# Fill for the last differential head from the output projection, in an encoder layer on one core

## The chip, the cores and the metric

The kernel runs on one core of one Trainium2 chip. The metric is the device time of one execution in microseconds, as the median of three runs.

## The reference

One layer of an encoder on a sequence of 512 tokens of width 2048, in float32: an input projection shared by two groups of attention heads, one output projection, and a SwiGLU network. Both halves are normed, shifted, scaled and gated by a condition `c`.

```
mod = silu(c) @ w_ada + b_ada;  sh1, sc1, gt1, sh2, sc2, gt2 = split(mod, 6)
h = rms_norm(x, g_norm1) * (1 + sc1) + sh1
q_d, k_d, v_d, cq, ckv, k_pe = split(h @ w_in)
a_out = rms_norm(differential_attention(norm(q_d), norm(k_d), v_d, lam, rel_bias))   # 8 heads, two softmaxes each
q_m = rms_norm(cq) @ w_q_b;  k_nope, v_m = split(rms_norm(ckv) @ w_kv_b)
b_out = latent_attention(rope(norm(q_m)), rope(norm([k_nope, k_pe])), v_m)            # 8 heads
x = x + gt1 * (concat(a_out, b_out) @ w_out)
h2 = rms_norm(x, g_norm2) * (1 + sc2) + sh2
x = x + gt2 * ((silu(h2 @ w_gate) * (h2 @ w_up)) @ w_down)
```

## The kernel before

All large products are made of three: each float32 operand is split into a high part and a low part (type fp32r), and `mm3` (L241) issues high by high, low by high and high by low into one PSUM bank. Such a **triple** of 512 columns is the unit in which this text counts. Activations lie transposed, 16 k-tiles of 128 x 512; the tokens are four row blocks of 128.

**Weights.** `weight_plan` lists all weight chunks in the order in which TensorE uses them. `Weights.get` hands out chunk i, splits chunk i+1 (ScalarE casts the high part, L90; VectorE or POOL subtracts for the low part, L98) and has SP load chunk i+2 (L74, L78). There are three raw buffers and two of each part. The output weights alternate between VectorE and POOL for the low part (`OUT_SPLIT`), those of the latent projections go to POOL.

**Order of the work.** TensorE keeps the order in which the program is written (`ORDERED`); for the other engines a scheduler chooses at build time. Attention runs head by head through lists of steps: `DIFF_STEPS` for the eight differential heads, `MLA_STEPS` for the eight latent heads. In them s, t, v, o, e and n are the scores of a row block, the transposes of the probabilities, the product with the values, the operands of the next head, the transposes of the finished output of the head before, and the start of the next head's norms. F and F1 are places for other work. There `between` lets a `Filler` take products from `projections` until so many microseconds of them are issued (`DIFF_FILL`, `MLA_FILL`, split over the places of a head), and lets `side_work` take one or two steps. A step of the side work in the latent heads loads a 128 x 512 piece of w_ada (L308) and accumulates it on VectorE (L312, L315): the second modulation's scales and shifts, 39 steps for each group of four k-tiles.

**What `projections` yields.** First what is left of the input projection, then `latents`, then for each of four pairs of latent heads `mla_project` (16 triples of 384 columns for the queries, 8 of 512 for keys and values). `out_half(b)` is the part of the output projection's column block b that needs only the differential heads: k-tiles 0 to 7, 32 triples, into the four banks of `acc`, and for b = 2 and 3 copied out into four slots (`half`). Before, it stands behind pairs 1 and 3. After each pair the generator yields 0, which ends a filling place, until the pair's first head has started and the last differential head's output exists:

```
if pr in (1, 3):
    yield from out_half({1: 2, 3: 3}[pr])
while pr not in started or mixT[H - 1] is None:
    yield 0
```

`mixT[H - 1]` is made in step e of the first latent head. Behind the last pair comes `out_half(0)`; behind the last head `fill.finish` issues all that is left, and the other parts of the output projection follow. The step lists run one head behind for t and v: a latent head's stretch, from its first score product to that of the next, holds its own scores, the transposes and values of the head before and the operands of the next.

**Buffers.** `slot` tiles (2 KB per partition, `N_SLOTS` of them) hold x, the split activations, operands, outputs, the halves and the pieces of w_ada.

Of the kernel before, what the change touches and what calls it, by code (L numbers as in the profile page):

```python
# [32 lines left out]


ORDERED = {mybir.EngineType.PE}
N_SLOTS = 45
T2_BUFS = 4
FIRST = 5

# [98 lines left out]
def weight_plan(a):  # L138
    w_in = a["w_in"][0]
    qkv = w_in[:, 0:3 * H * P].rearrange("(k p) (s n) -> p k s n", p=P, s=3)  # L140
    plan = []

    def rows(w, r0, nk, c0, n):
        return w[r0:r0 + nk * P, c0:c0 + n].rearrange("(k p) n -> p k n", p=P)

    def add_in(h, j):
        plan.append((("in", h, j), [2, 384], qkv[:, 2 * j:2 * j + 2, :, h * P:(h + 1) * P],
                     "dve" if h < FIRST else "pool"))

    for k0, nk in BLOCKS:  # L150
        for h in range(FIRST):
            for j in range(k0 // 2, (k0 + nk) // 2):
                add_in(h, j)
    for h in range(FIRST, H):
        for j in range(KC // 2):
            add_in(h, j)
    c0 = 3 * H * P
    for i in range(2):
        for j in range(KC // 4):
            plan.append((("cq", i, j), [4, 256], rows(w_in, j * 512, 4, c0 + i * 256, 256), "pool"))  # L160
    for j in range(KC // 2):
        plan.append((("ckv", j), [2, 320], rows(w_in, j * 256, 2, c0 + QL, 320), "pool"))

    def add_out(b, j0, j1):
        for j in range(j0, j1):
            plan.append((("out", b, j), [2, 512], rows(a["w_out"][0], j * 256, 2, b * 512, 512), OUT_SPLIT if j < 4 and b != 1 else "dve"))

    for pr in range(4):
        for j in range(2):
            plan.append((("qb", pr, j), [2, 384], rows(a["w_q_b"][0], j * 256, 2, pr * 384, 384), "pool"))  # L170
        plan.append((("kvb", pr), [2, 512], rows(a["w_kv_b"][0], 0, 2, pr * 512, 512), "pool"))
        if pr == 1:
            add_out(2, 0, 4)
        elif pr == 3:
            add_out(3, 0, 4)
    add_out(0, 0, 8)
    add_out(1, 0, 8)
    add_out(2, 4, 8)
    add_out(3, 4, 8)

    for j in range(STRAIGHT):
        for k4 in range(4):
            for n in ("gate", "up"):
                plan.append(((n, j, k4), [4, 256], rows(a["w_" + n][0], k4 * 512, 4, j * 256, 256), "dve"))
    return plan
# [14 lines left out]
def hybrid_layer(ctx, tc, a, out):  # L200
# [758 lines left out]
    def out_half(b):  # L959

        pss = [bank("acc", "ps_o") for _ in range(NT)]
        yield from project(pss, mixT, 512, [("out", b, j) for j in range(4)], 0, H, last=(b > 1), fine=True)
        if b > 1:
            half[b] = [slot("half", F32) for _ in range(NT)]
            for t in range(NT):
                act.copy(out=half[b][t], in_=pss[t])
        else:
            half[b] = pss
# [11 lines left out]
    def projections():  # L980
# [9 lines left out]
        yield from latents()  # L990
        for pr in range(4):
            yield from mla_project(pr)
            if pr in (1, 3):
                yield from out_half({1: 2, 3: 3}[pr])
            while pr not in started or mixT[H - 1] is None:
                yield 0
        yield from out_half(0)

# [473 lines left out]
GATE_EARLY = True  # L1472
START_FILL = 5.2
DIFF_STEPS = "s0 F s1 n F t0 F e s2 v0 F t1 F s3 v1 F t2 F o0 v2 t3 F o1 v3 F"
DIFF_FILL = (26.0, 26.0, 26.0, 26.0, 26.0, 26.0, 26.0, 26.3)
DIFF_SIDE = (1, 2, 1, 2, 1, 2, 1, 1)
MLA_SIDE = (1, 2)
MOD_EARLY = 8
MOD_PACE = (2.0, 2.4, 2.7, 1.5)
MLA_STEPS = "s0 F t0 e F1 t1 s1 v0 F t2 F1 v1 t3 s2 F v2 F1 o0 v3 F o2 o3 s3 o1 F1"  # L1480
MLA_FILL = (16.0, 15.7, 16.0, 0.2, 14.1, 19.0, 3.3, 12.8)


_INS = ["x", "c", "rel_bias", "w_ada", "b_ada", "g_norm1", "w_in", "g_q_diff", "g_k_diff", "lambda_vecs", "g_subln",
# [35 lines left out]
```

## Time and profile before

| | |
|---|---|
| three runs | 2253.54, 2254.41, 2261.16 us; median 2254.41 us |
| profiled execution | 2254.27 us, its span 2252.5 us |
| TensorE busy | 2178.6 us, 97% of the span |
| VectorE busy | 1648.1 us, 73% |
| ScalarE busy | 942.6 us, 42% |
| POOL busy | 262.7 us, 12%, all of it in the first 975 us |
| granted TensorE clock, mean | 0.996 of full speed |

Attention lies between about 200 and 755 us of the span, the latent heads from 542 us on. The network behind it takes the rest, with TensorE busy throughout. A busy TensorE says little by itself: the ends of matmuls are modelled, and a share over the whole span hides stretches of some 20 us. The windows view gives busy time, idle time as what is left, and the granted clock for stretches of one's own choice; those below begin and end with a head's first score product.

### The profile page before, as it was taken

The page shows a single profiled execution, that of the slowest core. Times are in us where ns is not written, and L with a number is a line of the kernel's source. Part 1 is how long each engine was busy: PE and PEld are TensorE (multiplying, and loading weights), DVE is VectorE, ACT ScalarE, POOL GpSimd, SP SyncE. Part 2 cuts the span into 40 slices and gives each one's busy share as a digit, 9 for nine tenths or more (in the row PEclk, how much of TensorE's full clock was granted, in tenths as well). Part 3 has the DMA queues.
Part 4 walks back from the last instruction along what each step waited for, and adds up shares of the span by engine and source line. Part 5 has one row for each costly group of instructions (what it writes and reads, how often), then busy time and mean ns, then how long its engine had stood idle before and what let it go on. Part 6 is the DMA issues. An engine that isn't in the chain of part 4 may idle for free.

```text
span 2252.5 us, 35369 instructions
## 1 busy us (share of the span) xinstructions
PE 2178.6 (97%) x13906; PEld 2000.5 (89%) x13906; DVE 1648.1 (73%) x2362; ACT 942.6 (42%) x1567; POOL 262.7 (12%) x408
## 2 busy tenths in 40 slices
PE   3899999998989999999999999999999999999999
PEld 3899998998777788899999999999999888888887
DVE  5997888868988687867777777777777677443554
ACT  4434555566555334534444444444444522221221
POOL 0003444345554000000000000000000000000000
PEclk9999999999999999999999999999999999999999
DMA  9995355422442684523333333333334686333443
GB/s 284 302 292 169 83 154 158 134 87 86 158 139 96 247 295 159 159 85 118 117 118 117 132 122 122 114 118 116 122 123 131 219 296 224 99 127 99 154 149 103
DMA packets 270826, 345.00 MB, mean 153 GB/s; under 512 B 15005, under 2 KB 171142, under 8 KB 270530
## 3 DMA queue, kind: packets, MB, share of 16 engines
q1 hardware_dynamic: 267864, 338.18, 46.5%
q10 hardware_dynamic: 2794, 4.55, 0.5%
q8 instruction: 109, 1.79, 0.3%
q14 instruction: 59, 0.48, 0.1%
HBM read 322.71 MB, written 19.96 MB: 152 GB/s over the span
## 4 chain that ended last, share of the span: by engine, by line
PE 67%; DVE 1%; DMA 0%; ACT 0%; issue 0%; POOL 0%; SPq 0%; DVEq 0%
PE ps_d L243 7%; PE ps_d L244 7%; PE ps_d L242 7%; PE ps_X L1285 5%; PE ps_X L1283 5%; PE ps_X L1284 5%; PE ps_W L1285 3%; PE ps_W L1283 3%; PE ps_W L1284 3%; PE ps_Y L1285 2%; PE ps_Z L1285 2%; PE ps_o L242 2%; PE ps_o L244 2%; PE ps_o L243 2%; PE ps_Y L1283 2%; PE ps_Z L1283 2%
## 5 line engine op out<-in xcount | busy, mean ns | idle before, releaser
L90 ACT CAST hi<-raw 128x1024 fp32r<-128x1024 f32 (+2 forms) x228 | 221.2, 970 | 479.2 <-PE ps_d L243 262.7
L98 DVE TENSOR_TENSOR lo<-raw,hi 128x1024 fp32r<-128x1024 f32 (+2 forms) x215 | 242.6, 1129 | 217.3 <-ACT hi L90 213.5
L1266 ACT CAST wh<-wr 128x1024 fp32r<-128x1024 f32 x160 | 168.2, 1051 | 245.3 <-PE ps_X L1284 69.2
L1285 PE MATMUL ps_X<-comb,wl 128*128 128x256 f32 x960 | 269.4, 281 | 0.0
L1283 PE MATMUL ps_X<-comb,wh 128*128 128x256 f32 x960 | 268.6, 280 | 0.0
L1284 PE MATMUL ps_X<-comb,wh 128*128 128x256 f32 x960 | 267.1, 278 | 0.0
L1249 DVE TENSOR_TENSOR wl<-wr,wh 128x1024 fp32r<-128x1024 f32 x160 | 195.6, 1222 | 76.5 <-ACT wh L1266 76.2
L244 PE MATMUL ps_d<-lo,ax 128*128 128x512 f32 x640 | 249.0, 389 | 0.0
L243 PE MATMUL ps_d<-hi,ax 128*128 128x512 f32 x640 | 249.0, 389 | 0.0
L242 PE MATMUL ps_d<-hi,ax 128*128 128x512 f32 x640 | 249.0, 389 | 0.0
L242 PE MATMUL ps_in<-hi,hh 128*128 128x384 f32 (+2 forms) x704 | 234.9, 334 | 3.3 <-ACT hh L397 1.3
L243 PE MATMUL ps_in<-hi,hl 128*128 128x384 f32 (+2 forms) x704 | 229.2, 326 | 4.3 <-DVE hl L403 4.3
L244 PE MATMUL ps_in<-lo,hh 128*128 128x384 f32 (+2 forms) x704 | 229.2, 326 | 3.4 <-DVE lo L98 3.4
L1266 ACT CAST wh<-wt 128x1024 fp32r<-128x1024 f32 x120 | 126.4, 1053 | 196.0 <-PE ps_X L1284 118.5
L1249 DVE TENSOR_TENSOR wl<-wt,wh 128x1024 fp32r<-128x1024 f32 x120 | 146.7, 1223 | 80.5 <-ACT wh L1266 80.3
L1283 PEld LDWEIGHTS ps_X<-comb,wh 128*128 128x128 f32 x960 | 180.5, 188 | 0.0
L1284 PEld LDWEIGHTS ps_X<-comb,wh 128*128 128x128 f32 x960 | 180.5, 188 | 0.0
L1285 PEld LDWEIGHTS ps_X<-comb,wl 128*128 128x128 f32 x960 | 180.2, 188 | 0.0
L1285 PE MATMUL ps_W<-comb,wl 128*128 128x256 f32 x640 | 179.6, 281 | 0.0
L1283 PE MATMUL ps_W<-comb,wh 128*128 128x256 f32 x640 | 179.2, 280 | 0.0
L1284 PE MATMUL ps_W<-comb,wh 128*128 128x256 f32 x640 | 178.1, 278 | 0.0
L242 PEld LDWEIGHTS ps_d<-hi,ax 128*128 128x128 f32 x640 | 120.2, 188 | 25.0
(324 smaller groups left out, 5330.6 us busy)
## 6 DMA issues: line engine op xcount, KB each, us to landing
raw<-in_w_down_dram SPq DMA_DIRECT2D x88, 512.0 KB
araw<-in_w_ada_dram SPq DMA_DIRECT2D x80, 512.0 KB
wr<-in_w_gate_dram SPq DMA_DIRECT2D x40, 1024.0 KB
wr<-in_w_up_dram SPq DMA_DIRECT2D x40, 1024.0 KB
ada<-in_w_ada_dram SPq DMA_DIRECT2D x128, 256.0 KB
raw<-in_w_in_dram SPq DMA_DIRECT2D x128, 192.0 KB
raw<-in_w_out_dram SPq DMA_DIRECT2D x32, 512.0 KB
x<-in_w_ada_dram SPq DMA_DIRECT2D x64, 256.0 KB
```

The lines of the kernel that those rows point to most:

```text
L90: nc.scalar.copy(out=hi[:, :n], in_=raw[:, :n])
L98: e.tensor_tensor(out=lo[:, :n], in0=raw[:, :n], in1=hi[:, :n].bitcast(F32), op=ALU.subtract)
L242: pe.matmul(o, ah, bh, start=start, stop=False)
L243: pe.matmul(o, al, bh, start=False, stop=False)
L244: pe.matmul(o, ah, bl, start=False, stop=stop)
L1249: dve.tensor_tensor(out=out, in0=x, in1=y, op=ALU.subtract)
L1266: act.copy(out=hi, in_=src)
L1283: pe.matmul(ps[bk], wh[:, k], c[:, 0], start=first and k == 0, stop=False, skip_group_check=True)
L1284: pe.matmul(ps[bk], wh[:, k], c[:, 1], start=False, stop=False, skip_group_check=True)
L1285: pe.matmul(ps[bk], wl[:, k], c[:, 0], start=False, stop=k == 7, skip_group_check=True)
```

## The change

`out_half(2)` moves from behind the second pair to behind the first, `out_half(3)` from behind the fourth to behind the third. The first of them no longer waits for the last differential head as a whole: it issues the triples of about six of its eight k-tiles, those that need the outputs of heads 0 to 5, and then yields 0 until the eighth head's output exists. The wait behind each pair is now only for its first head to start. `DIFF_FILL` of the last differential head rises from 26.3 to 38 us, `MLA_FILL` has other numbers. `N_SLOTS` is 51 instead of 45, and the kernel asks for a DMA scratch of 1024 bytes.

```diff
--- before.py
+++ after.py
@@ -33,7 +33,7 @@
 
 
 ORDERED = {mybir.EngineType.PE}
-N_SLOTS = 45
+N_SLOTS = 51
 T2_BUFS = 4
 FIRST = 5
 
@@ -169,9 +169,9 @@
         for j in range(2):
             plan.append((("qb", pr, j), [2, 384], rows(a["w_q_b"][0], j * 256, 2, pr * 384, 384), "pool"))
         plan.append((("kvb", pr), [2, 512], rows(a["w_kv_b"][0], 0, 2, pr * 512, 512), "pool"))
-        if pr == 1:
+        if pr == 0:
             add_out(2, 0, 4)
-        elif pr == 3:
+        elif pr == 2:
             add_out(3, 0, 4)
     add_out(0, 0, 8)
     add_out(1, 0, 8)
@@ -990,9 +990,16 @@
         yield from latents()
         for pr in range(4):
             yield from mla_project(pr)
-            if pr in (1, 3):
-                yield from out_half({1: 2, 3: 3}[pr])
-            while pr not in started or mixT[H - 1] is None:
+            if pr == 0:
+                first, due = out_half(2), 0.0
+                for t in first:
+                    yield t
+                    due += t
+                    while due > 6 * 12 * 512 * 0.000424 - 1 and mixT[H - 1] is None:
+                        yield 0
+            elif pr == 2:
+                yield from out_half(3)
+            while pr not in started:
                 yield 0
         yield from out_half(0)
 
@@ -1472,13 +1479,13 @@
 GATE_EARLY = True
 START_FILL = 5.2
 DIFF_STEPS = "s0 F s1 n F t0 F e s2 v0 F t1 F s3 v1 F t2 F o0 v2 t3 F o1 v3 F"
-DIFF_FILL = (26.0, 26.0, 26.0, 26.0, 26.0, 26.0, 26.0, 26.3)
+DIFF_FILL = (26.0, 26.0, 26.0, 26.0, 26.0, 26.0, 26.0, 38.0)
 DIFF_SIDE = (1, 2, 1, 2, 1, 2, 1, 1)
 MLA_SIDE = (1, 2)
 MOD_EARLY = 8
 MOD_PACE = (2.0, 2.4, 2.7, 1.5)
 MLA_STEPS = "s0 F t0 e F1 t1 s1 v0 F t2 F1 v1 t3 s2 F v2 F1 o0 v3 F o2 o3 s3 o1 F1"
-MLA_FILL = (16.0, 15.7, 16.0, 0.2, 14.1, 19.0, 3.3, 12.8)
+MLA_FILL = (21.0, 4.0, 21.0, 16.0, 16.5, 7.0, 5.0, 5.0)
 
 
 _INS = ["x", "c", "rel_bias", "w_ada", "b_ada", "g_norm1", "w_in", "g_q_diff", "g_k_diff", "lambda_vecs", "g_subln",
@@ -1504,7 +1511,7 @@
     import concourse.bacc as _bacc
     from concourse.bass_utils import run_bass_kernel_spmd as _run
 
-    nc = _bacc.Bacc("TRN2", target_bir_lowering=False, num_devices=1)
+    nc = _bacc.Bacc("TRN2", target_bir_lowering=False, num_devices=1, dynamic_dma_scratch_size=1024)
     arrays, aps = {}, {}
     given = {n: np.ascontiguousarray(inputs[n]) for n in _INS}
     given.update(_constants())
```

**TensorE, the end of the last differential head** (ps_s: scores, ps_z: product with the values, ps_aT: transposed probabilities, ps_qT and ps_kT: operands of the first latent head, ps_o: output projection). Before:

```order
L756 MATMUL ps_z<-v,aTh 128x256 x4
L759 MATMUL ps_z<-v,aTl 128x128 x4
L749 MATMUL ps_aT<-ident,pm 128x128 x4
L726 MATMUL ps_s<-k_5873,q_5865 128x512
L727 MATMUL ps_s<-klo,q_5865 128x512
L726 MATMUL ps_s<-k_6006,q_5998 128x512
L727 MATMUL ps_s<-klo,q_5998 128x512
L756 MATMUL ps_z<-v,aTh 128x256 x4
L759 MATMUL ps_z<-v,aTl 128x128 x4
L749 MATMUL ps_aT<-ident,pm 128x128 x4
L903 MATMUL ps_qT<-ident,qm 128x128 x4
L903 MATMUL ps_kT<-ident,kn 128x128 x4
```

After, from the same value product of the first row block (L759 behind the third score step) on:

```order
L759 MATMUL ps_z<-v,aTl 128x128 x4
L242 MATMUL ps_o<-hi,mh 128x512
L243 MATMUL ps_o<-hi,ml 128x512
L244 MATMUL ps_o<-lo,mh 128x512
L242 MATMUL ps_o<-hi,mh 128x512
L243 MATMUL ps_o<-hi,ml 128x512
L244 MATMUL ps_o<-lo,mh 128x512
L242 MATMUL ps_o<-hi,mh 128x512
L243 MATMUL ps_o<-hi,ml 128x512
L244 MATMUL ps_o<-lo,mh 128x512
```

The list goes on with four more triples, the transposes of the second row block, six triples, and only then the fourth score step. No triple stood here before.

**TensorE, the start of the second latent head.** Before:

```order
L920 MATMUL ps_s<-klo,q_6667 128x512
L242 MATMUL ps_o<-hi,mh 128x512
L243 MATMUL ps_o<-hi,ml 128x512
L244 MATMUL ps_o<-lo,mh 128x512
L242 MATMUL ps_o<-hi,mh 128x512
L243 MATMUL ps_o<-hi,ml 128x512
L244 MATMUL ps_o<-lo,mh 128x512
L242 MATMUL ps_o<-hi,mh 128x512
L243 MATMUL ps_o<-hi,ml 128x512
L244 MATMUL ps_o<-lo,mh 128x512
L934 MATMUL ps_aT<-ident,pm 128x128 x4
```

After:

```order
L920 MATMUL ps_s<-klo,q_6787 128x512
L934 MATMUL ps_aT<-ident,pm 128x128 x8
L242 MATMUL ps_s<-kTh,qTh 128x512
L243 MATMUL ps_s<-kTh,qTl 128x512
L244 MATMUL ps_s<-kTl,qTh 128x512
L919 MATMUL ps_s<-k_6795,q_6787 128x512
L920 MATMUL ps_s<-klo,q_6787 128x512
L242 MATMUL ps_z<-aTh,v 128x512
L243 MATMUL ps_z<-aTh,v 128x512
L244 MATMUL ps_z<-aTl,v 128x512
L934 MATMUL ps_aT<-ident,pm 128x128 x4
```

The output triples between score products and transposes are gone from this head, in all 24 of them; in the new program the sixth latent head has none either.

**VectorE between the third and the fourth score reduction of a latent head** (L922 reduces a score block, L315 accumulates a piece of w_ada). Before, in the fourth latent head, which had no fill:

```order
L922 TENSOR_REDUCE st<-ps_s 128x1
L315 SCALAR_TENSOR_TENSOR ada<-ada,c_col 128x512
L925 TENSOR_TENSOR st<-st,rsq 128x1
L840 COPY kn<-ps_in 128x256
L315 SCALAR_TENSOR_TENSOR ada<-ada,c_col 128x512
L927 RECIPROCAL st<-st 128x1
L638 SCALAR_TENSOR_TENSOR qTl<-ps_qT,small,qTh 128x512
L928 TENSOR_SCALAR pm<-pm,st 128x512
L635 TENSOR_TENSOR ml<-ps_z,mh 128x512
L629 TENSOR_TENSOR v<-vr,v 128x128 x2
L922 TENSOR_REDUCE st<-ps_s 128x1
```

After, in the second latent head, which has none now (the row ahead of these is L922 of the third row block and L629, the row behind is L922 of the fourth):

```order
L315 SCALAR_TENSOR_TENSOR ada<-ada,c_col 128x512
L925 TENSOR_TENSOR st<-st,rsq 128x1
L638 SCALAR_TENSOR_TENSOR qTl<-ps_qT,small,qTh 128x512
L315 SCALAR_TENSOR_TENSOR ada<-ada,c_col 128x512
L927 RECIPROCAL st<-st 128x1
L635 TENSOR_TENSOR ml<-ps_z,mh 128x512
L928 TENSOR_SCALAR pm<-pm,st 128x512
L315 SCALAR_TENSOR_TENSOR ada<-ada,c_col 128x512
L635 TENSOR_TENSOR q_7031<-ps_q,q_7031 64x512
L315 SCALAR_TENSOR_TENSOR ada<-ada,c_col 128x512
L635 TENSOR_TENSOR klo<-ps_k,k_7039 64x512
L315 SCALAR_TENSOR_TENSOR ada<-ada,c_col 128x512
```

Two accumulations stood there in the head without fill, five stand there now.

## Rows read from the trace of the kernel before

**Rows 1.** the page, section 1: busy us of each engine, share, instructions

```profile
PE 2178.6 (97%) x13906; PEld 2000.5 (89%) x13906; DVE 1648.1 (73%) x2362; ACT 942.6 (42%) x1567; POOL 262.7 (12%) x408
```

**Rows 2.** windows, one per head from 515.9 on: D, L1 to L8, the tail

```profile
core 0: us, PE busy (x) PEld busy (x) DVE busy (x) ACT busy (x) POOL busy (x), PEclk, DMA share, GB/s
515.90:542.30 26.40, 22.28 (x122) 19.70 (x121) 24.59 (x62) 19.57 (x52) 22.43 (x46) 0.87 0.38 129
542.30:567.70 25.40, 22.72 (x121) 19.61 (x120) 21.70 (x42) 14.18 (x32) 11.46 (x19) 1.00 0.35 118
567.70:597.10 29.40, 28.11 (x136) 22.68 (x137) 27.41 (x47) 12.05 (x24) 20.97 (x26) 1.00 0.48 156
597.10:626.60 29.50, 29.48 (x156) 25.42 (x155) 26.62 (x51) 18.62 (x41) 13.47 (x18) 1.00 0.39 127
626.60:648.80 22.20, 16.38 (x83) 12.39 (x81) 19.14 (x43) 10.64 (x24) 13.07 (x22) 0.92 0.30 97
648.80:676.20 27.40, 26.71 (x137) 23.75 (x138) 24.79 (x50) 16.37 (x36) 9.66 (x16) 0.94 0.58 175
676.20:708.00 31.80, 31.47 (x152) 25.36 (x151) 30.39 (x52) 14.43 (x30) 19.81 (x22) 1.00 0.44 147
708.00:725.50 17.50, 16.89 (x96) 13.62 (x94) 12.91 (x31) 11.32 (x24) 2.38 (x1) 1.00 0.10 33
725.50:749.00 23.50, 23.43 (x109) 18.87 (x110) 11.94 (x30) 10.27 (x21) 2.40 (x1) 1.00 0.15 44
749.00:756.00 7.00, 6.57 (x33) 4.36 (x32) 3.72 (x9) 3.48 (x8) 0.00 (x0) 1.00 0.97 344
```

**Rows 3.** TensorE's timeline, end of D: start, us, instruction, idle before

```profile
531.13 0.56 PE L759 MATMUL ps_z<-v,aTl 128*128 128x128 f32 x4
...
535.15 1.09 PE L749 MATMUL ps_aT<-ident,pm 128*128 128x128 f32 x4 [3.46 <-DVE cf L735]
...
543.66 0.49 PE L775 MATMUL ps_zT<-anti,z 128*128 128x128 f32 x3
...
545.90 0.33 PE L775 MATMUL ps_zT<-anti,z 128*128 128x128 f32 x1 [1.75 <-POOL z L769]
```

**Rows 4.** TensorE's timeline in L1 and L2, first products of following triples; L7, ada products

```profile
549.85 0.34 PE L242 MATMUL ps_in<-hi,cqh 128*128 128x384 f32 x1
...
550.37 0.33 PE L242 MATMUL ps_in<-hi,cqh 128*128 128x384 f32 x1
...
584.51 0.40 PE L242 MATMUL ps_o<-hi,mh 128*128 128x512 f32 x1
...
585.20 0.39 PE L242 MATMUL ps_o<-hi,mh 128*128 128x512 f32 x1
...
714.52 1.84 PE L354 MATMUL ps_ada<-ones,ada 128*128 128x1 f32 x16
```

**Rows 5.** waits of TensorE, 60:515, then 515.9:570: us, times, longest

```profile
PE ps_in L244 <- DVE lo L98: 3.4, 4, 1.9
...
PE ps_s L242 <- ACT kTh L637: 0.9, 1, 0.9
```

**Rows 6.** VectorE's groups in L3, L4 (two rows), L6: xcount, busy us, mean ns, idle before

```profile
L315 DVE SCALAR_TENSOR_TENSOR ada<-ada,c_col 128x512 f32<-128x512 f32 x10 | 7.5, 748 | 0.1
...
L315 DVE SCALAR_TENSOR_TENSOR ada<-ada,c_col 128x512 f32<-128x512 f32 x6 | 4.8, 808 | 0.0
...
L355 DVE TENSOR_TENSOR G<-ps_ada,small 128x4 f32<-128x4 f32 x1 | 0.2, 163 | 1.2 <-PE ps_ada L354 1.2
...
L315 DVE SCALAR_TENSOR_TENSOR ada<-ada,c_col 128x512 f32<-128x512 f32 x13 | 12.7, 977 | 0.1
```

**Rows 7.** POOL: low parts (page, section 5 and lines), then its timeline, L3 and L4

```profile
L98 POOL TENSOR_TENSOR lo<-raw,hi 128x1024 fp32r<-128x1024 f32 (+1 forms) x13 | 30.6, 2357 | 88.8 <-ACT hi L90 88.8
...
621.12 0.25 POOL L861 TENSOR_SCALAR rsq<-rsq 128x8 f32<-128x8 f32 x1
...
642.99 1.06 POOL L884 TENSOR_TENSOR kn<-kn,rsk 128x256 f32<-128x256 f32 x1 [3.79 <-DVE kn L840]
```

## The prediction

> **What bounds the kernel now.** I read the page first: TensorE is busy for 2178.6 of 2252.5 us [rows 1], so only its 74 idle us and its slow-clock time can be won, apart from work that the change does not touch. The windows view, cut at the first score product of each head, then shows where they lie [rows 2]: D is the last differential head (515.9 to 542.3), L1 to L8 are the latent heads after it. In L3, L6 and L8 TensorE is busy for nearly the whole stretch. In D it idles 26.4 - 22.28 = 4.1 us at a granted clock of 0.87, and in L4 22.2 - 16.38 = 5.8 us at 0.92. A mean of 0.87 between the two levels, 1.2 and 2.4 GHz, costs (1 - 0.87) x 26.4 = 3.4 us. These two stretches have one thing in common: no fill, the projection products that stand between the steps of attention elsewhere. The timeline of D names its stalls: the transposes of the third row block wait 3.46 us for VectorE and the last output transpose 1.75 us for POOL [rows 3].
>
> The same rows show the second bound. VectorE is busy for 26.62 of 29.5 us in L3 and for 30.39 of 31.8 in L6. It evicts for the attention, and between that it accumulates the second modulation (the ada tiles, L312 and L315), 12 of them per head until L6. TensorE's own work for one latent head is only 31.47 - 29 x 0.69 = 11.5 us: L6 holds 29 fill triples, and a triple of 512 columns takes 0.69 us (584.51 to 585.20), one of 384 columns 0.52 us [rows 4]. So a latent head without fill is not as short as TensorE's work but as long as VectorE's.
>
> **What moves, part by part.** The instructions are the same ones in both programs, so the sum is over stretches: for each, the change of its length less the change of its fill (a triple that leaves a stretch runs elsewhere at 0.69 us). Fill in triples, from the order of instructions:
> - D: 4 of 384 and 8 of 512 columns, now 23 more of 512 (+15.9 us); L1: 26, now 7 more (+4.8).
> - L2: 24, now none (-16.6); L3: 30, now 7 more (+4.8); L4: none, now 19 (+13.1).
> - L5: 25, now 24; L6: 29, now none (-20.0); L7: 5, now 8; L8: 20, now 8; behind the heads 53, now 60.
>
> So two stretches lose their shortage of fill and two get one.
>
> D: the 4.1 + 3.4 = 7.5 us go, as 7 triples now stand between the second and the third score step and 13 (9 us) between the third and the fourth, time in which VectorE catches up. The fill stops at the 23rd triple, waiting for the last head's output, so the steps behind keep short waits: the first output product for the banks of the pair's keys, the last values for their transposes. I put 1.0 us on them (0 to 4). Gain **6.5**. L1: the 1.75 us wait for POOL stays; the 0.93 us wait for the key's eviction [rows 5] is covered by 4 triples now. Gain **0.8**.
>
> L2, without fill, resembles the old L4, in which VectorE was busy 19.14 us with 7 accumulations. The new order has 12 in L2: five more at 0.81 us [rows 6] make 23.2; the three small sums behind the ada products, 0.4, are not there: 22.8. Of L4's 3.06 us of idle VectorE 1.2 was a wait for those products; of the rest I leave 1.5. So 24.3 us. L2 was 29.4 - 16.6 = 12.8 without its fill: loss **11.5**. L6 also has 12, but no leftover sums and copies of a projection (1.6 us): 22.7, against 31.8 - 20.0 = 11.8: loss **10.9**. For both, 14 us is the lower end (L7 of before, 17.5 less 3.5 of fill, had one accumulation) and 29 the upper (slow accumulations and POOL, below); I take the values next to L4, the only head without fill.
>
> L3 and L7 begin after a starved stretch, as L5 did, whose clock of 0.94 cost 0.06 x 27.4 = 1.6 us: with small waits, losses **1.8** and **1.4**. L4 becomes 11.5 own + 1.8 ada products [rows 4] + 0.7 waits instead of 22.2: gain **8.2**. L5 now has VectorE work of about 26.2 us (24.79, less one accumulation, plus two sums and two copies and what is left of the values), 12.4 beyond its fill against 12.9: gain **0.5**. L8 with 8 triples instead of 20 runs close to its chains: loss **0.5**.
>
> Sum: -6.5 - 0.8 + 11.5 + 1.8 - 8.2 - 0.5 + 10.9 + 1.4 + 0.5 = **+10.1 us**, on the profiled execution's 2254.27: 2264.4. The median of the runs is 0.14 us above that execution.
>
> Edits at no cost, and their cover. Four output weights are loaded and split before the second pair's: two low parts fall to POOL at 2.36 us each [rows 7], in front of the first pair's keys and between the rows' z. POOL was busy 22.43 us in D, and 27.2 fits into the 36 us that D becomes; without that room the first latent head's key transposes would be late by up to 4.7. On SP those loads stand ahead of the second pair's; the DMA share of D is 0.38. The copies of the four half sums move on ScalarE from L3 to L1, where it is busy 14.18 of 25.4 us. Six more slots let some ada loads go earlier, ahead of weights whose split TensorE waited 3.4 us for before this region [rows 5]: between -2 and +2, taken as 0. The smaller DMA scratch adds no instruction: 0. The Trainium skill (SBUF — State Buffer, SBUF size: 192, 224, or 256?) counts that scratch as the ring of DMAs that GpSimd issues; POOL's list holds no DMA in this kernel.
>
> POOL may also end last in L2, where it prepares a pair's keys. In the old L4 it did the same from 621.12, 5.5 us ahead of that stretch, to 644.05, 17.5 us into it [rows 7], and L4's length holds whatever that cost. A low part on POOL in between would add up to 2.4: 0 to 3 us, taken as 0.
>
> **The rivals.** *VectorE's accumulations trail behind* (the other side): if they slip out of L2 and L6 the two take some 14.5 us each, their losses become 1.7 and 2.7, the slow clock after them goes too, and the sum is -11.1: 2243.2. The point that decides is 18.4 us for each, where gains and losses are equal. For it: in L7 TensorE lost little with 3.5 us of fill. Against it: VectorE's instructions stand in one list, and the new list puts five accumulations between the third and the fourth score step of L2. Chance 0.12, a third of it so far down or further.
>
> *The accumulations stretch*: in L3 one took 748 ns, in L6, where POOL was busy 19.81 us, 977 [rows 6]. With 12 at 977 L2 and L6 grow by 2.0 each, and the slow clock inside them adds about 1.5 each (L4 lost 0.08 x 22.2 = 1.8 to it): +7, 2271.4. Chance 0.25. The Trainium skill (SBUF — State Buffer, Who interferes with whom) says why an accumulation could wait: two operands from SBUF collide with a GpSimd instruction that reads SBUF, and the later one blocks until the other is done. By that rule the stretch follows POOL's activity, which in L2, with a pair's keys to do, would be L6's of before; the forecast's 0.81 is the row of a head with POOL busy 13.07 us.
>
> *The fill in D does not do what it should*: the first output products wait for their split weights, or the stall moves to the fourth block's transposes; if about 4 us of the 7.5 stay, 2268.4. Chance 0.13.
>
> **How the numbers follow.** My forecast has 0.50, for about 2257 to 2267. The range takes in the trailing case down to half way and the stretched case with 3.6 us of waits more: 2249 to 2275. About 0.5%, 11.3 us of the median, is what a measurement of this kernel can tell from no change; the bounds are 2243.1 and 2265.7. Slower by more: the stretched case almost whole, 0.24, of the weak fill 0.10 and 0.06 of the forecast's upper end: 0.40. Faster by more: 0.05. Within: 0.55.
>
> **What the new profile would show.** Right: D filled, its clock near 1.0, no wait of more than 1 us before its last steps; L2 and L6 at 22 to 26 us with VectorE over 90% busy, TensorE at half its time, and waits for VectorE's low parts; L4 under 28 us and without its idle 5.8. Wrong: L2 or L6 under 19 us; a wait for output weights in D; a granted clock below 0.9 over L3 or L7 would push it to the upper end.

## Result, and the profile after

The changed kernel takes 2278.48 us (median of four runs, 2276.06 to 2279.55), the kernel before 2254.31 (four runs): a ratio of 1.0104, 95% interval 1.0087 to 1.012. It is slower, as forecast, but by some 24 us and not by 10; the profiled execution (2276.06 us) is 21.8 us above that of before. 2278.5 lies above the forecast's range.

The page's busy line of the changed kernel beside [rows 1] shows nearly the same work, TensorE 5.5 us more (products run at the slow clock last longer):

```profile
PE 2184.1 (96%) x13906; PEld 2003.4 (88%) x13906; DVE 1648.1 (72%) x2362; ACT 944.3 (42%) x1567; POOL 261.1 (11%) x408
```

The windows view of the changed kernel, one line per head with the columns of [rows 2] (D, L1 to L8; the last line ends at the first product behind the heads):

```profile
516.23:552.12 35.89, 35.61 (x190) 29.92 (x190) 26.43 (x62) 22.03 (x54) 27.39 (x48) 1.00 0.29 96
552.12:581.43 29.31, 27.56 (x141) 23.61 (x141) 22.60 (x41) 15.87 (x34) 11.35 (x17) 1.00 0.40 126
581.43:603.63 22.20, 15.72 (x65) 11.41 (x64) 21.71 (x43) 11.02 (x24) 16.30 (x27) 0.85 0.61 207
603.63:644.96 41.33, 37.10 (x175) 31.85 (x176) 33.45 (x63) 19.05 (x40) 17.17 (x24) 0.92 0.27 92
644.96:673.72 28.76, 26.37 (x138) 21.54 (x136) 19.11 (x37) 14.36 (x30) 13.59 (x16) 1.00 0.29 97
673.72:705.41 31.69, 27.50 (x136) 23.72 (x137) 27.10 (x53) 16.33 (x36) 9.88 (x13) 0.89 0.42 135
705.41:728.10 22.69, 14.00 (x65) 10.08 (x65) 20.69 (x40) 9.65 (x21) 12.96 (x24) 0.92 0.52 179
728.10:749.43 21.33, 19.01 (x105) 15.29 (x105) 15.51 (x40) 9.69 (x22) 0.00 (x0) 1.00 0.00 1
749.43:775.84 26.41, 22.32 (x101) 16.90 (x101) 16.52 (x36) 12.62 (x27) 2.34 (x1) 0.94 0.26 82
```

D is full now, at full clock. L2 and L6 have VectorE busy for 98% and 91% and TensorE idle for 6.5 and 8.7 us. The lines that the forecast did not expect are L3, L5 and L8: all three hold fill, and all have over 4 us of idle TensorE and a clock of 0.92, 0.89 and 0.94. Taken with the forecast's own rule, the change of a length less the change of its fill:

| stretch | length before, after | fill | net | forecast |
|---|---|---|---|---|
| D | 26.4, 35.9 | +15.9 | -6.4 | -6.5 |
| L1 | 25.4, 29.3 | +4.8 | -0.9 | -0.8 |
| L2 | 29.4, 22.2 | -16.6 | +9.4 | +11.5 |
| L3 | 29.5, 41.3 | +4.8 | **+7.0** | +1.8 |
| L4 and L5 | 49.6, 60.5 | +12.4 | **-1.5** | -8.7 |
| L6 | 31.8, 22.7 | -20.0 | +10.9 | +10.9 |
| L7 | 17.5, 21.3 | +2.1 | +1.7 | +1.4 |
| L8, to the first product behind the heads | 29.7, 26.4 | -8.3 | **+5.0** | +0.5 |

The last row ends at the first product of the output projection behind all score and value products, 755.17 in the old trace and 775.84 in the new one. The sum is +25.2, and 0.3 lies ahead of D. Behind the heads seven more triples (+4.8) stand, but that part grew by 1.1 us only, from 1497.3 to 1498.5; the 3.7 between lead back to the 21.8. About 1 us of them lies in the output projection, and the rest in the network behind it, where the change moves nothing; no experiment here separates that from the scatter of one execution. L4 and L5 stand together because [rows 2] cut them at 648.8, in the middle of a stall: the first score product of L5 stands at 647.40 in that trace, and it and the low-part product behind it waited 1.16 and 1.39 us.

What stalls the start of L5 now is in TensorE's timeline of the changed kernel (start, us, instruction, idle before):

```profile
666.99 0.39 PE L244 MATMUL ps_o<-lo,mh 128*128 128x512 f32 x1
...
670.78 0.66 PE L903 MATMUL ps_kT<-ident,kn 128*128 128x128 f32 x4
673.72 0.50 PE L242 MATMUL ps_s<-kTh,qTh 128*128 128x512 f32 x1 [2.28 <-ACT kTh L637]
...
677.24 0.79 PE L244 MATMUL ps_s<-kTl,qTh 128*128 128x512 f32 x1 [2.72 <-DVE kTl L638]
```

The last fill triple of L4 ends at 667.4, so nothing stands between the transposes of the keys (670.78) and the scores that need them, evicted: 5.0 us. The engines that evict were busy elsewhere. ScalarE copied the four sums of `out_half(3)`, just finished, until 671.34, and then did two casts and a block of probabilities that had queued behind the copies, all ahead of the high part of the keys. VectorE's list had an accumulation that waited for its piece of w_ada ahead of the low part:

```profile
669.29 2.05 ACT L966 COPY half<-ps_o 128x512 f32<-128x512 f32 x4
...
672.92 0.74 ACT L637 ACTIVATE kTh<-ps_kT,small 128x512 fp32r<-128x512 f32 x1
```

```profile
675.37 0.75 DVE L315 SCALAR_TENSOR_TENSOR ada<-ada,c_col 128x512 f32<-128x512 f32 x1 [2.03 <-DMA ada<-in_w_ada_dram]
676.44 0.75 DVE L638 SCALAR_TENSOR_TENSOR kTl<-ps_kT,small,kTh 128x512 fp32r<-128x512 f32 x1
```

Why the piece came late stands in SP's rows: its wait between 664 and 672 us, then its timeline.

```profile
SPq L74 <- POOL lo L98: 8.1, 1, 8.1
```

```profile
661.42 8.95 SPq L74 DMA_DIRECT2D raw<-in_w_out_dram  x2
670.46 13.19 SPq L308 DMA_DIRECT2D ada<-in_w_ada_dram  x11
```

SP issues its loads in the order of its list. The second of the two output-weight loads waited 8.1 us for a raw buffer, until POOL had finished a low part, and the w_ada loads behind it could go out only at 670.46. VectorE started on the first piece 4.9 us later.

At the start of L3 it is the same place without copies and without the late load: VectorE does two accumulations (603.52 and 604.91), a low part and a reduction ahead of the low part of the keys (606.17). TensorE's waits in L3 (us in total, times, longest):

```profile
PE ps_s L244 <- DVE kTl L638: 2.6, 1, 2.6
PE ps_o L242 <- DVE kn L840: 1.6, 1, 1.6
PE ps_s L242 <- ACT kTh L637: 0.8, 1, 0.8
```

L8 loses its time near its end. Between its last scores and the transposes that need their probabilities stood three triples; now there is one, and TensorE waits. Before, then after:

```profile
749.64 0.77 PE L934 MATMUL ps_aT<-ident,pm 128*128 128x128 f32 x5 [0.19 <-DVE pm L928]
...
769.12 0.77 PE L934 MATMUL ps_aT<-ident,pm 128*128 128x128 f32 x5 [3.32 <-DVE pm L928]
```

### The profile page after: what moved, and what is told of

It is laid out like the page before. It is cut to its first block, busy times and chain, and to the rows that moved or that the text cites. A ratio compares the mean times of both kernels' runs of the same rounds, so it can differ in the third digit from the quotient of the medians.

```text
span 2274.3 us, 35337 instructions
## 1 busy us (share of the span) xinstructions
PE 2184.1 (96%) x13906; PEld 2003.4 (88%) x13906; DVE 1648.1 (72%) x2362; ACT 944.3 (42%) x1567; POOL 261.1 (11%) x408
## 4 chain that ended last, share of the span: by engine, by line
PE 84%; DVE 8%; DMA 3%; issue 2%; ACT 2%; POOL 1%; SPq 0%; ACTq 0%; DVEq 0%; POOLq 0%
PE ps_d L243 7%; PE ps_d L244 7%; PE ps_d L242 7%; PE ps_X L1290 5%; PE ps_X L1292 5%; PE ps_X L1291 5%; PE ps_in L242 4%; PE ps_in L243 4%; PE ps_in L244 4%; PE ps_W L1290 3%; PE ps_W L1292 3%; PE ps_W L1291 3%; PE ps_o L242 2%; PE ps_o L243 2%; PE ps_o L244 2%
```

## The experiments

A profile is one execution, and the time ahead of D scatters: D's first score product stands between 511.8 and 520.2 us in the profiles below. Stretches are compared therefore, and whole times by their ratio to the kernel before, with the 95% interval.

**Spread the fill evenly.** Changed kernel, one line:

```diff
-MLA_FILL = (21.0, 4.0, 21.0, 16.0, 16.5, 7.0, 5.0, 5.0)
+MLA_FILL = (10.0, 10.5, 12.4, 12.4, 12.4, 12.4, 9.0, 9.0)
```

> The changed kernel with the latent heads' fill spread evenly: 10, 10.5, then four times 12.4, 9, 9 us instead of 21, 4, 21, 16, 16.5, 7, 5, 5; everything else as changed. Theory A, starved heads: L2 and L6 of the changed kernel are as long as VectorE's list, and what VectorE has not done there trails into L3. Then a head without starvation takes 11.5 us of TensorE's own work and 10 to 13 us of fill, or VectorE's 23 to 25 us, whichever is longer: eight heads at 24 to 25.5, and the whole about 2252 to 2260, 18 to 26 us under the changed kernel's 2278, with no wait over 2 us at the start of L3. Theory B, late loads: SP issues w_ada loads behind an output-weight load that waits for its raw buffer, and VectorE waits for them, so that only a few us come from the spread: 2268 to 2275, and waits of 2 us for w_ada stay at the places where the third pair's weights are loaded.

2277.19 us, 1.0094 (1.0069 to 1.012): nothing won, and neither theory named the reason. L2 takes 37.1 us and L6 38.4. TensorE's and POOL's timelines in L2 of this kernel:

```profile
594.56 0.39 PE L244 MATMUL ps_in<-lo,ckvh 128*128 128x512 f32 x1
...
603.29 0.47 PE L650 MATMUL ps_k<-ident,kpt 128*128 128x128 f32 x1 [6.76 <-POOL kpt L886]
```

```profile
602.05 0.61 POOL L884 TENSOR_TENSOR kn<-kn,rsk 128x256 f32<-128x256 f32 x1
...
606.05 0.61 POOL L886 TENSOR_TENSOR kpt<-kpe,rsk 128x256 f32<-128x256 f32 x1
```

From the pair's last product (594.56) to its last key on POOL (606.66) are 12.1 us, through VectorE, ScalarE and POOL. The even spread issues that product right ahead of the next pair's first operands, and the chain lies bare. So the changed kernel's early fill in L1 and L5 has a use: it hides this chain, and the empty head is its price.

**Only the first move.** `out_half(2)` as changed, `out_half(3)` behind the fourth pair as before.

```diff
-        elif pr == 2:
+        elif pr == 3:
...
-MLA_FILL = (21.0, 4.0, 21.0, 16.0, 16.5, 7.0, 5.0, 5.0)
+MLA_FILL = (10.0, 10.5, 7.0, 7.0, 14.1, 19.0, 3.3, 12.8)
```

> Only the first of the two moves: out_half(2) in D and L1 as changed, out_half(3) behind the fourth pair as before, with before's fill for L5 to L8 and 10, 10.5, 7, 7 us in L1 to L4. Theory A: no head is without fill, D keeps its gain of 6.4, L1 to L4 hold 57 triples and take 22 to 24 us each, L5 to L8 are as before: 2248 to 2256, about the kernel before or a little better. Theory B: the output weights of the second half go back to their old place, so the 5 us at the start of L5 go as well; alone that would give about 2272.

2267.17 us, 1.0046 (1.0025 to 1.0068). It lies between the two theories. L5 is free of the stall, but L2 (36.9 us) and L4 (31.1) wait 14.3 us for POOL's keys, the same late pair. L8 has 20 triples again, and its transposes wait 0.9 us and not 3.3.

**Accumulations out of L2 and L6.**

```diff
-MLA_SIDE = (1, 2)
+MLA_SIDE = ((2, 2), (0, 0), (2, 2), (2, 2), (2, 2), (0, 0), (2, 2), (2, 2))
...
-                    between(MLA_FILL[g] / MLA_STEPS.count("F"), MLA_SIDE[i])
+                    between(MLA_FILL[g] / MLA_STEPS.count("F"), MLA_SIDE[g][i])
```

> The changed kernel with its fill, but no step of the second modulation in L2 and L6 and 16 instead of 12 in the other latent heads. Theory A: VectorE's list in L2 and L6 gets 12 accumulations (9 us) shorter, the two come down to 14 to 18 us each from 22.2 and 22.7, the 5 us at the start of L3 go, and the four more accumulations in the filled heads cost 0 to 2 us each: 2260 to 2270. Theory B: nothing in the loads changes for the better, 2275 to 2280; the wait for w_ada at the start of L5 stays or grows as more pieces are wanted per head.

2271.26 us, 1.0076 (1.0054 to 1.0098), between the ranges of the two theories. Windows of L2, L3, L5, L6:

```profile
585.42:603.09 17.67, 12.37 (x65) 8.93 (x63) 16.98 (x38) 10.69 (x24) 13.67 (x22) 1.00 0.43 145
603.09:642.73 39.64, 36.08 (x175) 30.35 (x176) 33.17 (x61) 18.15 (x39) 18.33 (x23) 0.96 0.33 109
671.51:707.52 36.01, 28.56 (x137) 24.35 (x137) 33.02 (x59) 17.02 (x39) 15.40 (x23) 0.88 0.60 198
707.52:724.63 17.11, 13.90 (x64) 10.65 (x65) 15.46 (x35) 9.43 (x21) 8.35 (x14) 0.86 0.30 97
```

L2 with L3 is 6.2 us shorter and L6 5.6: VectorE's list was the bound of L2 and L6. At the start of L3 the wait for the low part of the keys falls from 2.6 to 0.2 us, but further on the one for the copies of the third pair's keys grows from 1.6 to 3.4, and L3 still takes 39.6: what VectorE brings over from L2 is only a part of its loss. L5, with four accumulations more, pays 4.3 back.

**Four raw weight buffers** (49 slots), so that SP has no weight load in front of w_ada that waits for its buffer:

```diff
-N_SLOTS = 51
+N_SLOTS = 49
...
-            return self.pool.tile([P, 1024], F32, tag="raw", bufs=3, name="raw")
+            return self.pool.tile([P, 1024], F32, tag="raw", bufs=4, name="raw")
```

> The changed kernel with four raw weight buffers instead of three (and 49 slots instead of 51 to make room), so that SP does not stand at a weight load with w_ada loads behind it. The fourth buffer is there in the later stages too. Theory B: the 2.0 us that VectorE waits for w_ada at 673 us and the 5 us at the start of L5 go, and L5 comes back from 31.7 to some 27: 2271 to 2275. Theory A: VectorE's lists in L2 and L6 and the backlog into L3 are as before, 2276 to 2280.

2283.40 us, 1.0132 (1.0106 to 1.0158). The wait for w_ada ahead of L5 is still 1.65 us and the two waits of TensorE 2.29 and 2.17; L5 takes 34.1. But the edit did not take away what it was to test. SP used the fourth buffer for one more weight load and stood at the next, and its first load of w_ada went out at the same time as in the changed kernel:

```profile
655.02 15.39 SPq L74 DMA_DIRECT2D raw<-in_w_out_dram  x3
670.51 14.98 SPq L308 DMA_DIRECT2D ada<-in_w_ada_dram  x11
```

So the run does not speak against theory B, and SP's rows of the changed kernel speak for it, as far as the 2.0 us for w_ada go. What the two slots fewer cost is not known.

**The slots alone**, on the kernel before:

```diff
-N_SLOTS = 45
+N_SLOTS = 51
...
-    nc = _bacc.Bacc("TRN2", target_bir_lowering=False, num_devices=1)
+    nc = _bacc.Bacc("TRN2", target_bir_lowering=False, num_devices=1, dynamic_dma_scratch_size=1024)
```

> The kernel before with 51 slots and the DMA scratch of 1024 bytes, nothing else. The forecast put the slots at 0, between -2 and +2 us: 2252 to 2257, same as before. If instead earlier w_ada loads collided with weights or a later pool were worse placed, it would show here: over 2260.

2252.29 us, 0.9984 (0.9967 to 1.0): no measurable change, as forecast.

**Fill in L6 without a pause.**

```diff
-            while pr not in started:
+            while pr not in started and pr < 3:
```

> The changed kernel without the wait behind the fourth pair, so that out_half(0) starts in L6 and L6 has fill (its 7 us, some 10 triples that lie behind the heads otherwise) behind the pair's last product. Theory A', lost cover: L6 is long because nothing of TensorE stands beside VectorE's list and the pair's chain over VectorE, ScalarE and POOL to its first keys; fill put there is free. L6 stays at 22 to 25 us with 7 us more work in it, and the whole falls by 4 to 7 us: 2271 to 2275. Rival D, VectorE's list is full and fill only adds waits: L6 grows by the fill, 2277 to 2281.

2275.32 us, 1.0091 (1.0069 to 1.0113). L5 and L6:

```profile
671.93:705.82 33.89, 31.27 (x155) 27.17 (x155) 27.87 (x54) 16.42 (x36) 11.89 (x14) 0.90 0.43 144
705.82:729.37 23.55, 20.84 (x98) 16.37 (x97) 22.42 (x42) 11.03 (x23) 13.14 (x23) 0.93 0.47 169
```

L6 takes 11 triples (7.6 us) for 0.9 us more: fill in an empty head is nearly free once the pair is done. With six more in L5 and one less in L7, 16 triples or 11 us leave the part behind the heads, but much comes back there: TensorE's waits from 773 to 900 us hold one that the changed kernel does not have, for an output weight's low part:

```profile
PE ps_o L244 <- DVE lo L98: 4.0, 1, 4.0
```

**The second pair's projection in D**, with `out_half(2)` behind it and no pause behind the first and fourth pair:

```diff
-        if pr == 0:
+        if pr == 1:
             add_out(2, 0, 4)
...
-            if pr == 0:
+            if pr == 1:
                 first, due = out_half(2), 0.0
...
-            while pr not in started:
+            while pr not in started and pr in (1, 2):
...
-MLA_FILL = (21.0, 4.0, 21.0, 16.0, 16.5, 7.0, 5.0, 5.0)
+MLA_FILL = (10.4, 10.4, 16.0, 16.5, 14.5, 7.0, 7.0, 6.8)
```

(also 47 slots, 12 instead of 8 tiles each for rotated parts and for values)

> D filled by the second pair's projection (24 triples) instead of out_half(2), which stays behind that pair and fills L1 and L2; out_half(3) behind the third pair in L3 and L4; out_half(0) straight behind the fourth pair from L6 on; 47 slots, since four more tiles for keys and four for values are needed. Theory A': D keeps its gain, and every latent head has fill of 7 to 16 us while the keys of the next pair are made, so that no head is bound by VectorE or POOL alone: 2242 to 2252, the fastest so far. Rival D: VectorE is the bound of heads 23 to 25 us long wherever the fill stands, 2253 to 2260. Rival E: with two pairs prepared at once POOL is late with the first pair's keys at the end of D, and most of the gain of D goes: 2256 to 2265.

2274.33 us, 1.0085 (1.0064 to 1.0105). D is as full (1.8 us idle in 51.2), but its 38 us of fill took most of `out_half(2)` too: L1 and L2 are left with nine triples and lose 5.3 and 5.4 us, L2 at a clock of 0.76. That is a hole moved, so this run says nothing on the rest of its theory.

**The end of L4's fill later.**

```diff
-MLA_FILL = (21.0, 4.0, 21.0, 16.0, 16.5, 7.0, 5.0, 5.0)
+MLA_FILL = (21.0, 4.0, 21.0, 12.0, 20.5, 7.0, 5.0, 5.0)
```

> The changed kernel with 12 us of fill in L4 and 20.5 in L5 instead of 16 and 16.5, so that the last products of out_half(3), and the four copies of its sums on ScalarE (2.05 us), come in the middle of L5 and not just ahead of its first scores. Theory F, ScalarE's copies: the 2.28 us wait for the high part of the keys at the start of L5 goes, and with it most of the 5 us: 2273 to 2276. Theory B, what VectorE waits for is w_ada: the second wait of 2.7 us stays or moves, 2276 to 2280.

2275.79 us, 1.0092 (1.0064 to 1.012). L4 and L5, with the same products as in the changed kernel:

```profile
648.87:674.73 25.86, 25.86 (x139) 21.69 (x137) 20.21 (x37) 12.21 (x26) 10.74 (x15) 1.00 0.36 120
674.73:703.52 28.79, 25.75 (x137) 21.96 (x136) 26.70 (x55) 18.35 (x40) 12.64 (x14) 1.00 0.43 139
```

54.7 us instead of 60.5, both at full clock: the 5.0 us stall is gone, and most of this term's miss with it. Three things changed together. Two triples (1.5 us) now stand behind the key transposes; ScalarE copies two of the four sums behind the high part of the keys; and SP had one weight load ahead of w_ada and not two, sent the first piece at 668.75, and VectorE did not wait for it. The run does not say what each is worth. In this execution L6 and L7 took 3.4 us more at clocks of 0.79 and 0.85 (0.92 and 1.00 in the changed kernel), and the median moved less than the stretch.

**The three repairs together** (no accumulations in L2 and L6, later end of L4's fill, no pause).

> The changed kernel with three repairs together: no step of the second modulation in L2 and L6 (16 in L1, L3, L4, L7 and L8, 12 in L5); the fill of L4 and L5 as in the run with later copies (12 and 20.5 us); out_half(0) straight behind the fourth pair. If the excess of the changed kernel is the sum of what the single runs showed by stretch (L2 with L3 6.2, L4 with L5 5.8, L6 5 to 6 us, less some 7 us that the earlier out_half(0) gave back behind the heads), the whole is 2260 to 2268. If what is won in one stretch only moves to the next (VectorE full over the eight heads), it stays at 2269 to 2276.

2271.81 us, 1.0086 (1.0071 to 1.0101): they do not add up. With three repairs L5 takes 43.1 us, since VectorE, in its fixed order, waits there for a piece of w_ada, and the query operands of L6 wait behind it for 7.5. SP stood at an output-weight load again, 12.7 us for a low part on POOL, and sent the piece at 698.82:

```profile
703.46 3.37 DVE L315 SCALAR_TENSOR_TENSOR ada<-ada,c_col 128x512 f32<-128x512 f32 x1 [9.12 <-DMA ada<-in_w_ada_dram]
```

**Only the second move**, on the kernel before with 51 slots (`out_half(3)` behind the third pair, no pause behind the fourth):

```diff
-        elif pr == 3:
+        elif pr == 2:
             add_out(3, 0, 4)
...
-            if pr in (1, 3):
-                yield from out_half({1: 2, 3: 3}[pr])
-            while pr not in started or mixT[H - 1] is None:
+            if pr in (1, 2):
+                yield from out_half(pr + 1)
+            while (pr not in started and pr < 3) or mixT[H - 1] is None:
...
-MLA_FILL = (16.0, 15.7, 16.0, 0.2, 14.1, 19.0, 3.3, 12.8)
+MLA_FILL = (16.0, 15.7, 16.0, 13.0, 15.5, 10.0, 8.0, 8.0)
```

> Only the second of the two moves, on the kernel before with 51 slots: out_half(2) stays behind the second pair and D is unfilled as before; out_half(3) stands behind the third pair, out_half(0) straight behind the fourth; L4 gets 19 triples instead of none, L5 27, L6 16, L7 12. No latent head is without fill. Theory A': L4's 5.8 idle us and the slow clock of L4 and L5 (3.4) go, no head becomes starved: 2244 to 2251, faster than before. Rival G, the weights behind the heads come late (DMA busy there) and the lighter L7 and L8 give it back: 2252 to 2258.

2263.28 us, 1.0046 (1.0031 to 1.0061), above both forecasts. L4, L5, L6:

```profile
625.92:651.77 25.85, 25.85 (x139) 21.67 (x137) 20.76 (x41) 13.05 (x26) 18.08 (x23) 1.00 0.35 119
651.77:680.19 28.42, 27.50 (x147) 23.77 (x146) 24.25 (x45) 14.54 (x29) 8.12 (x7) 1.00 0.39 125
680.19:714.77 34.58, 25.83 (x114) 19.96 (x114) 27.41 (x55) 16.05 (x37) 20.09 (x31) 0.90 0.42 140
```

L4 with 19 triples has no idle time: 25.85 - 13.1 - 20.8 = -8.1, the forecast's term for L4. L6 has 16 triples and is 34.6 us long all the same. The fourth pair's last product is issued in it, at 697, and its keys follow at 711.

**The first pair's end later**, to fill D from the heads ahead, on the kernel before with 51 slots:

```diff
-DIFF_FILL = (26.0, 26.0, 26.0, 26.0, 26.0, 26.0, 26.0, 26.3)
+DIFF_FILL = (25.0, 25.0, 25.0, 25.0, 25.0, 25.0, 25.0, 33.3)
```

> The kernel before with 51 slots and one edit: the first seven differential heads get 25.0 instead of 26.0 us of fill, the last 33.3 instead of 26.3, so that D holds 16 triples of 384 and 8 of 512 columns instead of 4 and 8, and nothing of the order behind it is touched. If D's 7.5 us of idle and slow clock can be filled without emptying another stretch, this gives 3 to 6 us: 2247 to 2252. Rival H: the first pair's last product comes later in D, and its keys (a chain of some 12 us over VectorE, ScalarE and POOL, as the runs with even fill showed) are late for the first latent head: 2254 to 2262.

2259.83 us, 1.002 (1.0009 to 1.003), rival H: D takes 42.6 us, 5.5 of them a wait for the first pair's keys on POOL. D can be filled with work that no one waits for, not with the pair whose head comes next.

**The fourth pair done in L5**, otherwise as the second move alone:

```diff
-MLA_FILL = (16.0, 15.7, 16.0, 13.0, 15.5, 10.0, 8.0, 8.0)
+MLA_FILL = (16.0, 15.7, 16.0, 17.5, 18.5, 9.0, 7.0, 6.0)
```

> As the run with the second half early, but more fill in L4 and L5 (26 and 32 triples instead of 19 and 27), so that the fourth pair's last product is issued in L5 and not in L6; L6 keeps 14 triples, all of out_half(0). If L6's loss is the late pair (from the last product to the first key some 14 us over VectorE, ScalarE and POOL, with nothing left to hide it), L6 falls from 34.6 to 23 to 26 us with as much fill, L5 grows by 3 to 4 (more fill), L4 by 4.8, and the whole is 2250 to 2257. If L6 is bound by VectorE's list whatever TensorE has, it stays over 30 and the whole over 2260.

2259.93 us, 1.0024 (1.0012 to 1.0037). L6:

```profile
696.24:721.49 25.25, 22.12 (x107) 16.87 (x106) 25.19 (x47) 10.63 (x23) 15.79 (x20) 1.00 0.45 155
```

L6 falls from 34.6 to 25.3 us with 14 triples in it: the late pair was its length. The whole stays above its forecast; behind the heads the 4.0 us wait for a low part is there again.

**Both halves one pair earlier**, on the kernel before with 51 slots: `out_half(2)` in D and L1 as in the change, `out_half(3)` behind the second pair, no pause behind the fourth, `DIFF_FILL` ending in 38.0 and

```diff
+MLA_FILL = (20.5, 15.7, 16.0, 2.0, 14.1, 10.0, 7.0, 6.0)
```

> Both halves earlier by one pair than before: out_half(2) behind the first pair, in D and L1 as in the changed kernel, out_half(3) behind the second pair, so that L2 holds 23 triples as before; L4 is as empty as before; out_half(0) straight behind the fourth pair, so that L6 has 16. If the loss of the changed kernel is the empty heads L2 and L6, the gain of D and L1 (7.3 us) stays and the rest is as before, less 4 to 8 us that the earlier out_half(0) gives back in L6 and behind the heads: 2248 to 2257. If filling D costs something further on whatever stands in L2 (weights, slots, VectorE's accumulations pushed back), it is 2260 or more.

**The same with the third pair's last four triples in L3**, none in L4:

```diff
-MLA_FILL = (20.5, 15.7, 16.0, 2.0, 14.1, 10.0, 7.0, 6.0)
+MLA_FILL = (20.5, 15.7, 19.5, 0.2, 14.1, 10.0, 3.3, 8.0)
```

> As the run with both halves one pair earlier, but with 19.5 us of fill in L3 and none in L4, so that the third pair's last four triples are issued in L3; less of out_half(0) in L7. If the 35.6 us of L4 in that run are the late keys of the third pair, L4 falls to 21 to 24 us with the same number of products by its end, L3 grows by 3, and the whole is 2254 to 2268, some 15 to 25 us faster than with the four triples in L4. If they come from anything else in L4 (VectorE's list, slots, weights), L4 stays over 30 us and the whole over 2272.

The first takes 2281.28 us, 1.0115 (1.0097 to 1.0133), far above its forecast; the second 2265.96, 1.005 (1.0032 to 1.0068), within it. D and L2, then L3 and L4, of the first:

```profile
519.61:555.59 35.98, 35.72 (x190) 29.92 (x190) 26.38 (x62) 22.01 (x54) 27.38 (x48) 1.00 0.29 96
...
584.87:614.45 29.58, 27.39 (x135) 21.98 (x133) 25.00 (x47) 12.90 (x26) 18.57 (x22) 1.00 0.41 135
614.45:646.50 32.05, 28.99 (x153) 24.59 (x151) 26.10 (x47) 17.52 (x37) 9.82 (x9) 1.00 0.35 125
646.50:682.06 35.56, 23.16 (x93) 18.03 (x92) 19.91 (x50) 11.88 (x29) 15.35 (x31) 0.71 0.29 92
```

L3 and L4 of the second:

```profile
612.63:646.73 34.10, 31.32 (x165) 27.07 (x163) 28.98 (x54) 19.11 (x41) 13.68 (x18) 1.00 0.43 148
646.73:666.49 19.76, 15.64 (x81) 12.02 (x80) 18.44 (x37) 10.85 (x24) 13.05 (x22) 0.91 0.30 93
```

Four triples issued in L3 instead of L4 shorten L4 by 15.8 us and lengthen L3 by 2.1: TensorE waits 8.3 us for the third pair's keys on POOL in the L4 of the first, and not at all in that of the second. D keeps its gain to 0.1 us, and L2 with 23 triples is as long as before with 24. No version tried is faster than the kernel before by a measurable amount.

## Why the prediction was partly right

The direction was right, and so were the terms of D, L1, L2 and L6. Three other steps failed. The stretches add up to 15.1 us more than the forecast's +10.1: L3 has 5.2 of it, L4 with L5 7.2 and L8 4.5; L2 takes 2.1 off, and 0.3 lies in the others.

**D and L1.** Right to 0.1 us each: -6.4 and -0.9 against -6.5 and -0.8, with the clock at 1.00 and no wait of over 1 us in D's steps. The run with the halves in D and L2 repeats it.

**L2 and L6.** Right in size: 22.2 and 22.7 us against 24.3 and 22.7, VectorE over 90% busy. That VectorE's list is the bound, the premise, is shown by the run that takes the accumulations out (17.7 and 17.1). The exact hit in L6 is in part luck: the forecast had L2 1.6 us longer than L6, and it is 0.5 shorter. The rival in which the accumulations trail behind did not come: L2 holds eleven of its twelve. But eleven more fall into the first 21 us of L3, and the last of L2's and the first of these run ahead of the low part of its keys.

**L3 and L7 "with small waits, losses 1.8 and 1.4".** L7 measured 1.7. L3 is the first step that failed: +7.0. It was priced by the slow clock of the old L5 alone. Measured are 4.2 us of idle TensorE where there was none, in waits for its keys (0.8 and 2.6) and for the copies of the third pair's keys on VectorE (1.6), and a clock of 0.92 over 41.3 us, 3.3 us where 1.6 were put. (The two come to 7.5, since the price of the clock over the whole stretch takes in idle time too.)

**L4 and L5, -8.2 and -0.5.** The second step that failed, by 7.2 us together. The forecast gave L4 "0.7 waits" because it was filled, without asking where in L4 the fill ends: it ends ahead of the key transposes, just as ScalarE has four sums to copy and VectorE waits for w_ada, and the start of L5 lies bare for 5.0 us and then runs at a clock of 0.89. Moving the same products a little later gives 5.8 us back, and the run with the second move alone measures -8.1 for L4. The mechanism was right; the place within the head was not looked at, nor the output-weight loads that now stand on SP ahead of w_ada. A row that would have shown it is the old start of L5, 1.16 and 1.39 us of waits in the same place, which the cut at 648.8 hid inside L4.

**L8 "runs close to its chains", +0.5.** The third step that failed: +5.0. With one triple left behind its last scores, the chain from them to their transposes lies bare for 3.3 us. On the way ScalarE casts a weight first (1.04 us), and VectorE's last step takes 1.70 us, beside a low part on POOL, and not 0.48. The wait follows the fill: it is 0.2 to 0.9 us in the runs with 20 triples in L8, and 3.1 to 3.3 in the single repairs of the changed kernel, which leave L8 its eight triples.

**Slots and scratch, 0.** Right: 0.9984 (0.9967 to 1.0).

**The stretched accumulations** came half. In L2 and L6 one takes 886 and 834 ns, between the 748 and 977 of [rows 6] (VectorE's groups: xcount, busy us, mean ns, idle before):

```profile
L315 DVE SCALAR_TENSOR_TENSOR ada<-ada,c_col 128x512 f32<-128x512 f32 x10 | 8.9, 886 | 0.0
...
L315 DVE SCALAR_TENSOR_TENSOR ada<-ada,c_col 128x512 f32<-128x512 f32 x12 | 10.0, 834 | 1.8 <-DMA ada<-in_w_ada_dram 1.8
```

In L2 one of the ten, beside a low part on POOL, took 1.66 us and holds most of the difference.

What stays open: what of L3's loss remains when VectorE brings nothing over from L2 (5.3 us in the run without accumulations there), what each of the three causes at the start of L5 is worth, and why the clock in the empty heads differs between executions of nearly the same list, 0.92 over L6 in the changed kernel and 0.79 in the run with the later end of L4's fill.

## What to carry to other kernels

Fill that is moved has a place inside its head as well as an amount: look at what stands between the last transposes of operands and the first product that needs them, and between a head's last scores and their transposes, and how long the chain from a producer's last product to its first use is (12 to 14 us here), before moving either end. An engine with one fixed list, here VectorE, hands a shortage on to the next stretch, and a queue with one list, here SP, makes every load wait that stands behind one without a buffer; price the start of that stretch by its own waits and not by the clock alone. Cut stretches at the first product of a stage, not in its stall.

## What the runs showed of the hardware

The clock outlasts its cause. In L2 no wait of TensorE was longer than 2.1 us, and the granted clock was between 0.81 and 0.90 all through. Around the 2.6 us wait at the start of L3 it was 0.72, and in the full stretch behind it 0.62, between the 1.2 and 2.4 GHz levels, with TensorE busy for 5.10 of 5.10 us:

```profile
603.60:608.90 5.30, 2.65 (x7) 1.96 (x8) 5.19 (x11) 0.87 (x2) 0.00 (x0) 0.72 0.81 278
608.90:614.00 5.10, 5.10 (x23) 5.07 (x22) 3.49 (x8) 0.87 (x2) 0.00 (x0) 0.62 0.00 0
614.00:619.00 5.00, 5.00 (x31) 4.71 (x30) 4.08 (x4) 2.75 (x4) 2.81 (x2) 1.00 0.00 0
```

An accumulation takes longer beside POOL's work. In L6 of the changed kernel the six that start before POOL's last instruction (717.48, 1.06 us) take 0.93 us in the mean, the six behind it 0.735. From both sides, then one beside a low part on POOL (616.19 to 618.59) in L3:

```profile
715.38 1.09 DVE L315 SCALAR_TENSOR_TENSOR ada<-ada,c_col 128x512 f32<-128x512 f32 x1
...
719.07 0.73 DVE L315 SCALAR_TENSOR_TENSOR ada<-ada,c_col 128x512 f32<-128x512 f32 x1
...
616.75 2.38 DVE L315 SCALAR_TENSOR_TENSOR ada<-ada,c_col 128x512 f32<-128x512 f32 x1
```

The Trainium skill (SBUF — State Buffer, Who interferes with whom) states that a VectorE instruction with two SBUF inputs contends with a GpSimd instruction that reads SBUF. The trace agrees. The price here is about 0.2 us each beside POOL's short instructions, some 1.2 us for a head, and 0.9 and 1.6 us for the two accumulations of L2 and L3 that met a low part.
